# A one-core hybrid decoder step: the pairs' weight halves divided between GpSimd and VectorE, half of the convolutions moved to the down stage, and another border in front of the pairs

## The chip, the core and the metric

The kernel runs on one core of a Trainium2 chip. The core has a TensorE (PE, with its weight load shown as PEld), a VectorE (DVE), a ScalarE (ACT), a GpSimd (POOL) and a SyncE (SP), which issues nearly all transfers. Each engine takes its instructions in program order and waits on semaphores for the others. The metric is the device time of one execution in microseconds (us); lower is better.

## The reference, cut to what matters

One layer of a decoder over 1056 tokens: 1024 of a prompt and 8 sequences of 4. All data is float32. The part that the change touches is the last third, the feed-forward block with its causal depthwise convolution of width 3:

```python
def _conv_ffn(h, cbuf, w_up, b_up, conv_w, conv_b, w_down, b_down):
    L = h.shape[1]
    u = h @ w_up + b_up                                  # 1024 -> 5632
    ux = jnp.concatenate([cbuf.astype(u.dtype), u], axis=1)
    y = conv_b + ux[:, 0:L] * conv_w[0]
    for j in range(1, CONV_W):
        y = y + ux[:, j:j + L] * conv_w[j]
    a, g = y[..., :D_FF], y[..., D_FF:]                  # D_FF = 2816
    out = (jax.nn.gelu(a) * g) @ w_down + b_down         # 2816 -> 1024
    return out, ux[:, L:]
...
    h2 = _ln(x) * (1.0 + sc2) + sh2
    f, cbuf_new = _conv_ffn(h2, cbuf, w_up, b_up, conv_w, conv_b, w_down, b_down)
    x = _ln(ALPHA * x + g2 * f, ln2_g, ln2_b)
```

Ahead of it stand the input projection, the mLSTM, the windowed attention, the gated merge and the output projection, which the change leaves alone.

## The kernel before

**Number format.** A float32 operand is split into a rounded high part and a low part, and each product is three matmuls: high by high, high by low, low by high. The high part is a cast on ScalarE, the low part a subtraction on VectorE or GpSimd. So each block of weights costs a cast and a subtraction before TensorE can use it.

**Layout.** Activations lie as tiles of 128 features by 1056 tokens. There are 43 such tiles ("slots") on the chip, handed out and given back in order of age. A product over 1056 tokens is made in three pieces of 384, 384 and 288 tokens, each in one of three accumulation banks (L), which ScalarE or VectorE empties.

**The up stage.** The 44 column blocks of `w_up` (128 columns each) belong in twos: block j (it goes through gelu) and block 22 + j (it multiplies). Some are made directly (`up_direct`, 24 matmuls for each piece of tokens). The others go through `fast`: for a pair of blocks, a Strassen-like scheme with seven half-size products (numbered 1 to 7) in place of eight. Each product is 12 matmuls of 264 tokens for each of two halves of the tokens, so a pair is 168 matmuls. Products go to a ring of eight accumulation banks; VectorE adds them into the two output tiles (`fdst`), and ScalarE copies out product 1. The operands of the scheme, sums and differences of the activation's quarters, are made once ahead of the first pair (`tprep`, `t1_split`). The sums and differences of the weights are made for each pair: four sums of 128x512 (`sum`, L1447), seven casts (`high`, L1464), seven low parts (`low`, L1468). In this kernel the sums and all seven low parts are GpSimd's.

**Before and after the pairs.** Three pairs of blocks (j = 0, 1, 2) are made directly in front of the pairs, two (j = 20, 21) behind them, and 17 pairs go through the scheme. `history` loads the convolution's old inputs and transposes them; it runs between the direct blocks and the pairs.

**Convolutions.** `conv` takes one tile: a ScalarE pass (L1746), two VectorE passes over the prompt's tokens (L1750, L1752), and small operations for the sequences on VectorE (L1755 to L1757), ScalarE and GpSimd (L1748, L1758, L1759). In the pairs' stage `post` does both convolutions of each pair, gelu (L1773), the product (L1776), and stores one finished tile. For the five direct j, the raw tiles are stored, and the convolutions are made later.

**The down stage.** Chunks (one j, 128 rows of `w_down`) are taken in five groups (`KG`). `feed` loads a chunk, makes what is not yet made of it, and splits it into high (L1842) and low (L1844). `down_group` multiplies a group with its weights and adds into eight accumulators (`facc`, L1959; in the first group ScalarE writes them, L1957). The weights' low parts are GpSimd's here. The fourth group goes by pieces of tokens (`down_by_tokens`), so that finished rows are transposed and added to the residual (`pre`, L1898); the last group is multiplied row by row with the final norm (L2124 on).

**What sets the order.** The order is written by a planner at build time. Each three matmuls call `pulse(us)`, which moves a planner's clock forward. Side work (`tprep`, `post`, `feed`, ...) is written as generators in one queue (`sides`); `rate` says how many steps of the generator in front are taken for each planner's microsecond. `later(us, f)` issues f that much later. `operands(gi)` stands in front of each group: if the group's chunks are not yet made, it takes the steps of the queue at once, with no matmul between them.

Of the kernel before, what the change touches and what calls it, by code (L numbers as in the profile page):

```python
# [19 lines left out]
SEQ = 1024  # L20
# [13 lines left out]
RATE_T, RATE_U, RATE_V, RATE_D, RATE_P = 0.85, 0.75, 0.8, 0.8, 0.9  # L34
# [70 lines left out]
def hybrid_step(ctx: ExitStack, tc: tile.TileContext, I, O):  # L105
# [1265 lines left out]
    def tprep():  # L1371

        for kp in range(4):
# [4 lines left out]
            yield  # L1378
            e, o = quarters(hf[2 * kp]), quarters(hf[2 * kp + 1])
            S.dma_start(b12D[kp], e[:, :, 1, :])  # L1380
            V.tensor_tensor(e[:, :, 0, :], e[:, :, 1, :], e[:, :, 0, :], op=OP.subtract)
            yield
            V.tensor_tensor(e[:, :, 1, :], o[:, :, 1, :], e[:, :, 1, :], op=OP.subtract)
            V.tensor_tensor(o[:, :, 1, :], o[:, :, 1, :], e[:, :, 0, :], op=OP.subtract)
            yield
            V.tensor_tensor(o[:, :, 0, :], o[:, :, 0, :], o[:, :, 1, :], op=OP.subtract)
            t_ops[kp] = slot(F32R, name="thi"), slot(F32R, name="tlo")
            A.copy(t_ops[kp][0], hf[2 * kp + 1])
# [8 lines left out]
            V.tensor_tensor(t3_ops[kp][1], e[:, :, 1, :], t3_ops[kp][0].bitcast(F32), op=OP.subtract)
# [23 lines left out]
    class Pair:  # L1421
# [44 lines left out]
        def low(self, p):  # L1466
            hi, lo = self.halves(p)
            G.tensor_tensor(lo, self.src[p], hi.bitcast(F32), op=OP.subtract)  # L1468
# [272 lines left out]
    def conv(c, u, y):  # L1741
# [3 lines left out]
        us = tiny([128, 8, 6], "us", 6)  # L1745
        A.activation(y[:, :SEQ], u[:, :SEQ], AF.Identity, bias=b, scale=w[2])  # L1746
        A.copy(us[:, :, 2:6], to3(u[:, SEQ:]))
        G.tensor_copy(us[:, :, 0:2], aux["hist"][:, :, :, c])  # L1748
# [5 lines left out]
        ys = to3(y[:, SEQ:])  # L1754
        V.tensor_scalar(ys, us[:, :, 2:6], w[2], b, op0=OP.mult, op1=OP.add)  # L1755
        V.scalar_tensor_tensor(ys, us[:, :, 1:5], w[1], ys, op0=OP.mult, op1=OP.add)
        V.scalar_tensor_tensor(ys, us[:, :, 0:4], w[0], ys, op0=OP.mult, op1=OP.add)  # L1757
# [448 lines left out]
```

## Time and profile before

| | |
|---|---|
| time, median of 3 runs | 2018.43 us (2017.61 to 2020.57) |
| the profiled execution's own time | 2016.51 us |
| its span | 2014.8 us |
| busy: PE, DVE, ACT, POOL | 1914.2, 1085.8, 775.3, 670.7 us |
| mean granted clock of TensorE | 0.988 |
| data read, written | 165.74 MB, 53.49 MB |

The page splits the span in 40 slices of some 50 us. The up stage begins near 1150 us; the pairs run from about 1259 to 1666 us, the down stage from about 1720 us to the end. TensorE is busy nearly throughout, so the places to look at are the ones where it isn't: these have a row with an idle time in brackets in the timeline of TensorE, or less than the stretch's length in the table of windows.

### The profile page before, as it was taken

The numbers are of one execution on the slowest core, as the hardware profiler recorded it, in microseconds if no ns is written. First come the engines' busy times: TensorE is split into PE (matmuls) and PEld (weight loads), VectorE is DVE, ScalarE is ACT, GpSimd is POOL, SyncE is SP. The second block draws the span as 40 slices with busy tenths as digits, with TensorE's granted clock in tenths as the row PEclk, the third lists the DMA queues.
The fourth block names the chain that finished last, engine by engine and source line by source line (L and its number), as shares of the span: only waits on it lengthen the run. The fifth ranks groups of instructions, "written<-read, shape, count | busy, mean of one in ns | idle before, by whom it ended". The sixth has DMA issues, their size and how long they took to land. (4 is left out here: it accounts for less than half of the span.)

```text
span 2014.8 us, 33111 instructions
## 1 busy us (share of the span) xinstructions
PE 1914.2 (95%) x13005; PEld 1818.0 (90%) x13005; DVE 1085.8 (54%) x2281; ACT 775.3 (38%) x1613; POOL 670.7 (33%) x806
## 2 busy tenths in 40 slices
PE   6999999999999999999999999798988999999987
PEld 4899999999998999988999988788888889999975
DVE  5454444354643635312553566677777775315778
ACT  5444334343655555410322454233333334431331
POOL 2013324140213122000000442578887870222327
PEclk9999999999999999999999999899999999999999
DMA  9152423515121322695424142212222125323373
GB/s 285 46 148 24 128 69 83 121 31 133 33 86 43 100 65 65 219 346 175 131 64 115 74 128 95 66 64 75 74 65 75 64 75 180 119 95 114 108 246 131
DMA packets 230981, 219.35 MB, mean 109 GB/s; under 512 B 11377, under 2 KB 207137, under 8 KB 230793
## 3 DMA queue, kind: packets, MB, share of 16 engines
q1 hardware_dynamic: 230045, 216.63, 35.3%
q8 instruction: 102, 1.67, 0.4%
q10 hardware_dynamic: 780, 0.61, 0.1%
q14 instruction: 54, 0.44, 0.1%
HBM read 165.74 MB, written 53.49 MB: 109 GB/s over the span
## 5 line engine op out<-in xcount | busy, mean ns | idle before, releaser
L454 PE MATMUL L<-hhi,whi 128*128 128x384 f32 (+1 forms) x1600 | 525.7, 329 | 0.1
L454 PE MATMUL L<-hlo,whi 128*128 128x384 f32 (+1 forms) x1600 | 516.4, 323 | 0.0
L454 PE MATMUL L<-hhi,wlo 128*128 128x384 f32 (+1 forms) x1600 | 516.0, 322 | 0.0
L454 PEld LDWEIGHTS L<-hhi,whi 128*128 128x128 f32 x1600 | 301.0, 188 | 6.6 <-issue 4.8
L454 PEld LDWEIGHTS L<-hlo,whi 128*128 128x128 f32 x1600 | 301.4, 188 | 0.3
L454 PEld LDWEIGHTS L<-hhi,wlo 128*128 128x128 f32 x1600 | 300.9, 188 | 0.0
L432 DVE TENSOR_TENSOR wlo<-wraw,whi 128x1024 fp32r<-128x1024 f32 (+1 forms) x87 | 107.0, 1230 | 111.0 <-ACT whi L428 110.0
L454 PE MATMUL L<-mhi,whi 128*128 128x384 f32 (+1 forms) x432 | 144.2, 334 | 11.8 <-ACT u L1737 5.5
L299 POOL TENSOR_SCALAR rstd<-mv 128x1 f32<-128x1 f32 (+1 forms) x36 | 22.0, 610 | 398.3 <-DVE mv L308 374.9
L454 PE MATMUL L<-mhi,wlo 128*128 128x384 f32 (+1 forms) x432 | 141.8, 328 | 0.4 <-DVE wlo L432 0.4
L454 PE MATMUL L<-ahi,whi 128*128 128x384 f32 (+1 forms) x432 | 140.9, 326 | 1.0 <-DVE facc L1959 0.9
L454 PE MATMUL L<-mlo,whi 128*128 128x384 f32 (+1 forms) x432 | 141.8, 328 | 0.1
L454 PE MATMUL L<-ahi,wlo 128*128 128x384 f32 (+1 forms) x432 | 139.7, 323 | 1.8 <-POOL wlo L432 1.8
L454 PE MATMUL L<-alo,whi 128*128 128x384 f32 (+1 forms) x432 | 139.4, 323 | 0.0
L1468 POOL TENSOR_TENSOR fw<-fsum,fw 128x512 fp32r<-128x512 f32 x68 | 105.2, 1548 | 76.5 <-ACT fw L1464 76.5
L432 POOL TENSOR_TENSOR wlo<-wraw,whi 128x768 fp32r<-128x768 f32 (+2 forms) x27 | 53.7, 1995 | 193.4 <-ACT whi L428 167.7
L428 ACT CAST whi<-wraw 128x1024 fp32r<-128x1024 f32 (+2 forms) x114 | 113.4, 996 | 3.6 <-DMA wraw<-in_w_in 2.2
L454 PEld LDWEIGHTS L<-mhi,whi 128*128 128x128 f32 x432 | 83.1, 192 | 14.5 <-ACT u L1737 6.8
L1750 DVE SCALAR_TENSOR_TENSOR y<-fdst,vT,y 128x1023 f32<-128x1023 f32 x34 | 43.7, 1284 | 82.3 <-ACT y L1746 80.9
L1494 PE MATMUL L<-mhi,fw 128*128 128x264 f32 x400 | 79.1, 286 | 9.1 <-POOL fw L1468 9.1
L1464 ACT CAST fw<-fsum 128x512 fp32r<-128x512 f32 x68 | 41.9, 616 | 112.0 <-POOL fsum L1447 110.9
L454 PEld LDWEIGHTS L<-mhi,wlo 128*128 128x128 f32 x432 | 83.0, 192 | 0.9 <-DVE wlo L432 0.9
(538 smaller groups left out, 4446.4 us busy)
## 6 DMA issues: line engine op xcount, KB each, us to landing
wraw<-in_w_in SPq DMA_DIRECT2D x52, 512.0 KB
wada<-in_w_ada SPq DMA_DIRECT2D x44, 512.0 KB
fraw<-in_w_up SPq DMA_DIRECT2D x34, 512.0 KB
ld<-ff SPq DMA_DIRECT2D x27, 528.0 KB
ff<-y SPq DMA_DIRECT2D x17, 528.0 KB
wraw<-in_w_down SPq DMA_DIRECT2D x88, 64.0 KB
ff<-u SPq DMA_DIRECT2D x10, 528.0 KB
wraw<-in_w_up SPq DMA_DIRECT2D x10, 512.0 KB
```

Source lines behind the costliest of these rows:

```text
L299: G.tensor_scalar(r[:n], var, eps, None, op0=OP.add)
L428: A.copy(hi[:, :n], t[:, :n])
L432: self.low_by.tensor_tensor(lo[:, :n], t[:, :n], hi[:, :n].bitcast(F32), op=OP.subtract)
L454: T.matmul(ps[:, :nt], x[:, c], y[:, t0:t0 + nt], start=i == 0, stop=i == last)
L1464: A.copy(hi, self.src[p])
L1468: G.tensor_tensor(lo, self.src[p], hi.bitcast(F32), op=OP.subtract)
L1494: T.matmul(ps, x, y, start=kp == 0 and i == 0, stop=kp == 3 and i == 2)
L1750: V.scalar_tensor_tensor(y[:, 1:SEQ], u[:, :SEQ - 1], w[1], y[:, 1:SEQ], op0=OP.mult, op1=OP.add)
```

## The change

- **Weights of the pairs.** GpSimd keeps the four sums and the low parts of products 1 and 4; VectorE takes the low parts of products 2, 3, 5, 6 and 7.
- **Convolutions.** In the pairs' stage only block 22 + j is convolved and stored (`yD`). Block j is stored raw (`uD`) and is convolved in the down stage, where `feed` now loads two tiles for every chunk and does gelu and the product for all 22. In `conv`, the four small operations of GpSimd and one of VectorE become ScalarE's.
- **Border in front of the pairs.** Four pairs of blocks are direct ahead of the scheme instead of three, and 16 pairs go through it. `tprep` is written so that the cast and the low parts of one step stand behind the next step's sums; `history` is run inside it.
- **Groups.** The down stage's groups have 5, 5, 5, 3 and 4 chunks instead of 6, 5, 4, 3 and 4. `feed` is one generator over all of them; it starts a chunk only if at least `ROOM` = 9 slots are free, and the rates of the planner are others.

```diff
-RATE_T, RATE_U, RATE_V, RATE_D, RATE_P = 0.85, 0.75, 0.8, 0.8, 0.9
+RATE_T, RATE_U, RATE_V, RATE_D, RATE_P = 0.5, 0.5, 1.1, 1.1, 1.1
+ROOM = 9
...
-    ND, NE = 3, 2
+    ND, NE = 4, 2
...
-    KG = [6, 5, 4, 3, 4]
-    chunks_of = [[3, 4, 5, 6, 7, 8], [9, 10, 11, 12, 0], [13, 14, 15, 1], [16, 2, 20], [17, 18, 19, 21]]
+    KG = [5, 5, 5, 3, 4]
+    chunks_of = [[4, 5, 6, 7, 8], [9, 10, 11, 0, 20], [12, 13, 14, 1, 21], [2, 15, 16], [3, 17, 18, 19]]
...
+        for kp in range(5):
+            if kp < 4:
+                join(kp)
+            yield
+            if kp:
+                high(kp - 1)
+            if kp < 4:
+                e, o = quarters(hf[2 * kp]), quarters(hf[2 * kp + 1])
+                S.dma_start(b12D[kp], e[:, :, 1, :])
+                V.tensor_tensor(e[:, :, 0, :], e[:, :, 1, :], e[:, :, 0, :], op=OP.subtract)
+                V.tensor_tensor(e[:, :, 1, :], o[:, :, 1, :], e[:, :, 1, :], op=OP.subtract)
+            yield
+            if kp < 4:
+                V.tensor_tensor(o[:, :, 1, :], o[:, :, 1, :], e[:, :, 0, :], op=OP.subtract)
+                V.tensor_tensor(o[:, :, 0, :], o[:, :, 0, :], o[:, :, 1, :], op=OP.subtract)
+            yield
+            if kp:
+                low(kp - 1)
             yield
...
         def low(self, p):
             hi, lo = self.halves(p)
-            G.tensor_tensor(lo, self.src[p], hi.bitcast(F32), op=OP.subtract)
+            (G if p in (1, 4) else V).tensor_tensor(lo, self.src[p], hi.bitcast(F32), op=OP.subtract)
...
+        ys = to3(y[:, SEQ:])
         A.activation(y[:, :SEQ], u[:, :SEQ], AF.Identity, bias=b, scale=w[2])
         A.copy(us[:, :, 2:6], to3(u[:, SEQ:]))
-        G.tensor_copy(us[:, :, 0:2], aux["hist"][:, :, :, c])
+        A.activation(ys, to3(u[:, SEQ:]), AF.Identity, bias=b, scale=w[2])
+        A.copy(us[:, :, 0:2], aux["hist"][:, :, :, c])
+        A.copy(aux["ucol"][:, c, 0:2], u[:, SEQ - 2:SEQ])
+        A.copy(aux["ucol"][:, c, 2:18].rearrange("p (b j) -> p b j", b=8), to3(u[:, SEQ:])[:, :, 2:4])
...
-        V.tensor_scalar(ys, us[:, :, 2:6], w[2], b, op0=OP.mult, op1=OP.add)
...
-        G.tensor_copy(aux["ucol"][:, c, 0:2], u[:, SEQ - 2:SEQ])
-        G.tensor_copy(aux["ucol"][:, c, 2:18].rearrange("p (b j) -> p b j", b=8), us[:, :, 4:6])
...
     def post(c, u):
         y = slot(name="y")
         yield from conv(c, u, y)
         drop(u)
...
+        to_dram(yD, c, y)
...
+    def feed():
+        js, got = [j for c in chunks_of for j in c], {}
+        def load(n):
+            if n < len(js) and n not in got:
+                ds = [uD[js[n]], yD[22 + js[n]] if 22 + js[n] in yD else uD[22 + js[n]]]
+                got[n] = [slot(name="ld") for _ in ds]
+                for t, d in zip(got[n], ds):
+                    S.dma_start(t, d)
+        load(0)
+        yield
+        for n, j in enumerate(js):
+            while len(free_slots) < ROOM:
+                yield
+            load(n + 1)
+            yield
+            u, y2 = got.pop(n)
+            if 22 + j not in yD:
+                u2, y2 = y2, slot(name="y")
+                yield from conv(22 + j, u2, y2)
+                drop(u2)
+                yield
+            y = slot(name="y")
+            yield from conv(j, u, y)
...
+            A.activation(y, y, AF.Gelu_apprx_tanh)
+            yield
+            yield
+            V.tensor_tensor(y, y, y2, op=OP.mult)
...
+            A.copy(hi, y)
+            yield
+            V.tensor_tensor(lo, y, hi.bitcast(F32), op=OP.subtract)
...
+            if n == 9:
+                yield from gate_rows2()
+        yield from kept_rows()
...
     def ff_finisher(j):
-        return lambda blk_, z: sides.append(post(22 * blk_ + j, z))
+        return lambda blk_, z: sides.append(post(22 + j, z)) if blk_ else to_dram(uD, j, z)
...
-        sums = tprep()
-        for i in range(23):
-            if i == 5:
+        sums, past = tprep(), history()
+        for i in range(22):
+            if i in (0, 5, 10):
+                next(past)
+            if i == 6:
                 upairs[0].load()
-            if i in (10, 11, 22):
-                upairs[0].step((10, 11, 22).index(i) - 3)
+            if i in (15, 20):
+                upairs[0].step((15, 20).index(i) - 3)
             else:
-                next(sums)
-            yield
-        next(sums, None)
+                next(sums, None)
+            yield
+        upairs[0].step(-1)
```

Three places show what the change does to the order. First GpSimd, over one pair in the middle of the pairs' stage; `fsum` are sums of weights, `fw` the weights in two parts, `fraw` the weights as loaded. Before:

```order
L1447 TENSOR_TENSOR fsum_12968<-fraw_12799,fraw_12800 128x512
L1447 TENSOR_TENSOR fsum_12968<-fraw_12799,fsum_12931 128x512
L1758 COPY ucol_12337<-fdst_12815 128x2
L1759 COPY ucol_12337<-us 128x16
L1468 TENSOR_TENSOR fw_12971<-fraw_12799,fw_12971 128x512
L1748 COPY us<-cst 128x8x2
L1468 TENSOR_TENSOR fw_13008<-fsum_12968,fw_13008 128x512
L1468 TENSOR_TENSOR fw_13042<-fsum_12931,fw_13042 128x512
L1758 COPY ucol_12337<-fdst_12740 128x2
L1759 COPY ucol_12337<-us 128x16
L1468 TENSOR_TENSOR fw_13078<-fraw_12800,fw_13078 128x512
L1468 TENSOR_TENSOR fw_13113<-fsum_12968,fw_13113 128x512
```

and with the change, a whole pair (the line numbers are the changed kernel's):

```order
L1460 TENSOR_TENSOR fsum_14007<-fraw_13885 128x512
L1460 TENSOR_TENSOR fsum_14007<-fsum_14007,fraw_13884 128x512
L1460 TENSOR_TENSOR fsum_14047<-fraw_13884,fraw_13885 128x512
L1460 TENSOR_TENSOR fsum_14047<-fraw_13884,fsum_14007 128x512
L1481 TENSOR_TENSOR fw_14151<-fraw_13885,fw_14151 128x512
L1481 TENSOR_TENSOR fw_14209<-fraw_14117,fw_14209 128x512
```

A pair has gone from eleven large operations and six small ones on GpSimd to six large ones.

Second, VectorE of the changed kernel at the border between the second and the third group of the down stage. L1963 is the addition into the accumulators (each waits for a block of matmuls), L1767 to L1772 the convolution, L1864 the product behind gelu, L1870 the chunk's low part:

```order
L1963 TENSOR_TENSOR facc_17192<-L_72,facc_17192 128x288
L1767 SCALAR_TENSOR_TENSOR y_17843<-ld_17628,vT,y_17843 128x1023
L1769 SCALAR_TENSOR_TENSOR y_17843<-ld_17628,vT,y_17843 128x1022
L1771 SCALAR_TENSOR_TENSOR y_17843<-us,vT,y_17843 128x32
L1772 SCALAR_TENSOR_TENSOR y_17843<-us,vT,y_17843 128x32
L1767 SCALAR_TENSOR_TENSOR y_17855<-ld_17627,vT,y_17855 128x1023
L1769 SCALAR_TENSOR_TENSOR y_17855<-ld_17627,vT,y_17855 128x1022
L1771 SCALAR_TENSOR_TENSOR y_17855<-us,vT,y_17855 128x32
L1772 SCALAR_TENSOR_TENSOR y_17855<-us,vT,y_17855 128x32
L1864 TENSOR_TENSOR y_17855<-y_17855,y_17843 128x1056
L1870 TENSOR_TENSOR alo_17870<-y_17855,ahi_17869 128x1056
L1963 TENSOR_TENSOR facc_16654<-L_73,facc_16654 128x384
```

The whole last chunk of the third group, with both its convolutions, now stands between the last addition of one group and the first of the next. Before, additions of both groups follow each other there:

```order
L1959 TENSOR_TENSOR facc_17388<-L_71,facc_17388 128x384
L1959 TENSOR_TENSOR facc_17388<-L_72,facc_17388 128x288
L1959 TENSOR_TENSOR facc_16848<-L_73,facc_16848 128x384
```

Third, VectorE at the border between the fourth and the last group; `PG` is the first bank of the final products, L2133 the first operation that reads one:

```order
L1963 TENSOR_TENSOR facc_17192<-L_72,facc_17192 128x288
L1998 TENSOR_TENSOR facc_17192<-facc_17192,modT 128x32
L1767 SCALAR_TENSOR_TENSOR y_18886<-ld_18565,vT,y_18886 128x1023
L1769 SCALAR_TENSOR_TENSOR y_18886<-ld_18565,vT,y_18886 128x1022
L1771 SCALAR_TENSOR_TENSOR y_18886<-us,vT,y_18886 128x32
L1772 SCALAR_TENSOR_TENSOR y_18886<-us,vT,y_18886 128x32
L1864 TENSOR_TENSOR y_18886<-y_18886,ld_18566 128x1056
L1870 TENSOR_TENSOR alo_18901<-y_18886,ahi_18900 128x1056
L2133 TENSOR_TENSOR PG<-PG,gp_17267 128x512
```

Before, the first final product's rows follow the last addition directly. With the change, the last chunk's work stands in between.

More of the change, by code (lines that the diff above doesn't have):

```diff
@@ L1371, in tprep, with join @@
     def tprep():
-        for kp in range(4):
+        def join(kp):
             for k in (2 * kp, 2 * kp + 1):
@@ L1806, in hybrid_step, with kept_rows @@
     acts2 = []
-    def feed(gi):
-        js, got = chunks_of[gi], {}
+    def kept_rows():
+        ucol = aux["tile"]
+        uo = slot(name="uo")
+        for _ in range(4):
+            yield
+        for i in range(7):
+            n = 128 if i < 6 else 24
+            transpose(pd(i)[:n], ucol[:, i * 128:i * 128 + n])
+        A.copy(uo[:, :512], PD[0])
+        A.copy(uo[:, 512:768], PD[1][:, :256])
+        A.copy(uo[:24, 768:896], PD[1][:24, 256:384])
+        drop(ucol)
+        yield
+        for i in range(7):
+            n = 128 if i < 6 else 24
+            r0 = i * 128
+            for dst, a, b in (("p_conv", 0, 88), ("s_conv", 88, 792)):
+                p, q = max(r0, a), min(r0 + n, b)
+                if p < q:
+                    S.dma_start(dap(O[dst], (p - a) * 128, [[128, q - p], [1, 128]]),
+                                uo[p - r0:q - r0, i * 128:(i + 1) * 128])
+        drop(uo)
+        yield
+    def feed():
+        js, got = [j for c in chunks_of for j in c], {}
         def load(n):
             if n < len(js) and n not in got:
-                ds = [aD3[js[n]]] if js[n] in aD3 else [uD[js[n]], uD[22 + js[n]]]
+                ds = [uD[js[n]], yD[22 + js[n]] if 22 + js[n] in yD else uD[22 + js[n]]]
                 got[n] = [slot(name="ld") for _ in ds]
@@ L1831, in feed @@
                 yield
-                yield from conv(j, u, y)
-                drop(u)
-                yield
-                A.activation(y, y, AF.Gelu_apprx_tanh)
-                yield
-                yield
-                V.tensor_tensor(y, y, y2, op=OP.mult)
-                drop(y2)
-                yield
+            y = slot(name="y")
+            yield from conv(j, u, y)
+            drop(u)
+            yield
[3 more added lines that the diff above has]
+            V.tensor_tensor(y, y, y2, op=OP.mult)
+            drop(y2)
+            yield
             hi, lo = slot(F32R, "ahi"), slot(F32R, "alo")
@@ L1904, in pre @@
             drop(*facc)
-            sides.append(kept_rows())
     summed = []
@@ L1962, in down_group @@
         a = operands(gi)
-        sides.append(feed(gi + 1))
         for j in range(8):
@@ L1977, in down_by_tokens @@
         a = operands(gi)
-        sides.append(feed(gi + 1))
         for ti in range(3):
@@ L2060, in hybrid_step @@
     finish_sides()
-    sides.append(history())
     rate[0] = RATE_U
@@ L2079, in hybrid_step @@
     fast(upairs, up_end)
-    sides.append(feed(0))
+    sides.append(feed())
     rate[0] = RATE_V
```

63 lines of the change are left out of this document (6 added, 57 removed).

## The prediction

> **What bounds the kernel now.** I read the page first, then a table of windows cut at the stages' borders, then the chain of waits within the slow stages.
>
> ```profile
> span 2014.8 us, 33111 instructions
> ...
> 1210.00:1258.80 48.80, 44.43 (x275) 41.54 (x274) 32.67 (x50) 21.93 (x39) 10.54 (x10) 0.97 0.28 96
> 1258.80:1282.30 23.50, 10.19 (x58) 8.86 (x57) 15.83 (x17) 8.42 (x16) 9.99 (x7) 0.64 0.30 94
> ...
> 1300.00:1650.00 350.00, 317.58 (x2545) 311.23 (x2543) 262.08 (x375) 122.46 (x211) 278.82 (x252) 1.00 0.21 69
> ...
> 1673.40:1890.00 216.60, 216.60 (x1340) 216.45 (x1341) 89.92 (x121) 73.75 (x104) 47.54 (x46) 0.99 0.36 117
> 1890.00:1960.00 70.00, 58.54 (x342) 53.14 (x341) 47.22 (x72) 26.60 (x41) 19.27 (x13) 0.95 0.64 220
> ```
>
> The columns are the stretch, its length, the busy time of PE, PEld, DVE, ACT, POOL, the granted clock, the DMA share and GB/s. From 1673 to 1890 us, TensorE has no gap: it bounds the down stage, and VectorE has 127 us to spare. In the pairs (1300 to 1650) it lacks 32 us while GpSimd is busy for 279 of 350. In front of the pairs (1259 to 1282) it works 10 of 23.5 us, at 0.64 of its clock.
>
> What sets the pace of a pair is in the chain of waits and in the groups of that stretch:
>
> ```profile
> 1279.29 3.01 PE PD L1494 x12
> ...
> 1291.03 2.90 PE PD L1494 x24
> 1293.93 1.46 PE PE L1494 x12
> 1295.39 4.39 PE L L1494 x36
> 1299.78 1.50 PE PF L1494 x12
> ...
> 1341.71 1.30 POOL fw L1468
> ...
> 1364.96 1.29 POOL fw L1468
> ...
> 1673.39 116.82 PE L L454 x714
> ```
>
> ```profile
> L1468 POOL TENSOR_TENSOR fw<-fsum,fw 128x512 fp32r<-128x512 f32 x60 | 93.1, 1551 | 70.0 <-ACT fw L1464 70.0
> L1447 POOL TENSOR_TENSOR fsum<-fraw,fraw 128x512 f32<-128x512 f32 x15 | 34.3, 2286 | 0.0
> L1447 POOL TENSOR_TENSOR fsum<-fraw 128x512 f32<-128x512 f32 x15 | 19.2, 1279 | 0.0
> ...
> L1752 DVE SCALAR_TENSOR_TENSOR y<-fdst,vT,y 128x1022 f32<-128x1022 f32 x30 | 62.5, 2083 | 0.5
> L1750 DVE SCALAR_TENSOR_TENSOR y<-fdst,vT,y 128x1023 f32<-128x1023 f32 x30 | 38.5, 1284 | 78.9 <-ACT y L1746 78.9
> L1517 DVE SCALAR_TENSOR_TENSOR fdst<-L,vT,fdst 128x264 f32<-128x264 f32 x47 | 21.8, 485 | 0.4
> ```
>
> The same low part comes back every 23.25 us (1341.71 to 1364.96), which is the period of a pair. Where nothing holds it up, TensorE does 72 matmuls between 1291.03 and 1299.78, 0.1215 us each, so a pair's 168 need 20.4 us. GpSimd, which casts on ScalarE wait for and which waits for casts, costs 2.85 us in each pair. VectorE and GpSimd also slow each other: the two equal passes L1750 and L1752 take 1.28 and 2.08 us, the equal sums 1.28 and 2.29.
>
> **The pairs and the border in front.** First and last matmuls of this stage, and TensorE's waits around its start:
>
> ```profile
> L1494 PE MATMUL L<-mhi,fw x400: 278/284/391, 1283.6 to 1665.8; 128*128 128x264 f32 x134
> ...
> L1494 PE MATMUL PF<-mhi,fw x144: 278/285/393, 1258.8 to 1658.6; 128*128 128x264 f32 x144
> ```
>
> ```profile
> 1246.28 0.44 PE L454 MATMUL L<-mhi,whi 128*128 128x384 f32 x1 [0.95 <-ACT u L1737]
> ...
> 1253.98 0.40 PE L454 MATMUL L<-mhi,whi 128*128 128x288 f32 x1 [3.22 <-ACT u L1737]
> 1268.26 0.59 PE L1494 MATMUL PD<-thi,fw 128*128 128x264 f32 x1 [5.29 <-ACT thi L1388]
> ...
> 1277.13 1.62 PE L197 MATMUL PD<-cst,hraw 128*128 128x128 f32 x6 [6.77 <-DVE fdst L1504]
> ```
>
> The stage takes 1665.8 - 1258.8 = 407.0 us for 17 pairs, stalls at its start included. With the change GpSimd has six large operations a pair, at most 6 x 2.29 = 13.7 us, against a period of 20.4. VectorE loses one convolution, gelu's product and a small operation and gains five low parts. None of 512 columns stands on it yet; one of 528 does:
>
> ```profile
> 1236.25 0.70 DVE L1397 TENSOR_TENSOR tl<-hf,th 128x528 fp32r<-128x528 f32 x1
> ...
> 1859.29 0.25 DVE L1756 SCALAR_TENSOR_TENSOR y<-us,vT,y 128x32 f32<-128x32 f32 x1
> ```
>
> So 14 additions of 0.485 (6.8), five low parts of 0.70 (3.5), two passes of 1.28 (2.6), two small ones (0.5): 13.4 us. If each of the seven longer ones were slowed by 0.8 like L1752, it is 19. Both are under 20.4, so TensorE sets the pace. Of the waits this adds, the tightest is product 6's low part: it stands behind product 4's addition, with that pair's convolution behind it, and is wanted two products of 2.9 us later. In the 16 pairs, 16 x 20.4 = 326.4 us. The pair that becomes direct is 144 matmuls at 116.82/714 = 0.1636: 23.6. Together 350.0, a gain of **57.0**. For filling the first pair I take back **2**; the bounds are 0 and today's 13.6 us (5.29, 6.77, and the 1.55 by which twelve matmuls took 3.01 instead of 1.46 behind them). I stay near 0, since `tprep` and `history` now stand under three direct blocks. ScalarE's waits on `tprep` (0.95 and 3.22) go with the new spacing: **4.2**, at worst 0, if its casts of `fw` block the evacuations as today.
>
> **The down stage.** It makes 28 convolutions in place of 10, and 22 gelus and products in place of 5. Durations of each there, from the timelines of ScalarE and VectorE:
>
> ```profile
> 1822.20 1.09 ACT L1835 ACTIVATE y<-y 128x1056 f32<-128x1056 f32 x1 [17.03 <-DVE y L1757]
> ...
> 1825.44 1.25 DVE L1838 TENSOR_TENSOR y<-y,y 128x1056 f32<-128x1056 f32 x1
> 1826.77 1.08 ACT L1842 CAST ahi<-y 128x1056 fp32r<-128x1056 f32 x1 [2.86 <-DVE y L1838]
> 1827.70 0.56 DVE L1959 TENSOR_TENSOR facc<-L,facc 128x384 f32<-128x384 f32 x1 [1.02 <-PE L L454]
> 1828.17 1.25 DVE L1844 TENSOR_TENSOR alo<-y,ahi 128x1056 fp32r<-128x1056 f32 x1
> ...
> 1846.88 1.24 ACT L1746 ACTIVATE y<-ld,vT 128x1024 f32<-128x1024 f32 x1 [6.36 <-PE L L454]
> ...
> 1855.23 1.27 DVE L1750 SCALAR_TENSOR_TENSOR y<-ld,vT,y 128x1023 f32<-128x1023 f32 x1
> ```
>
> A convolution is 2 x 1.27 + 2 x 0.25 = 3.0 us on VectorE. Eighteen more and 17 more products of 1.25 are 76 us; with the 89.9 there it stays far under the stage, so in the mean it hides behind the matmuls. A chunk's own chain is 1.24 + 3.0 + 1.09 + 1.25 + 1.08 = 7.7, with hand-overs some 8.3 us. The planner gives it ten steps at 1.1, 9.1 of its microseconds. Its clock counts 1.32 for nine matmuls, which take 9 x 0.1636 = 1.47, so that is 10.1 us: enough. The loads double to two tiles a chunk, 1.08 MB in 10 us, 107 GB/s beside today's 117; 220 is reached a stage later.
>
> What doesn't hide are the group borders where the order has chunk work with no matmul between (the places shown with the change). The wait for nine free tiles puts them there: the feed idles until a group's tiles come back.
>
> - Up to first group: gelu, product, cast and low part of the fifth chunk stand behind the last evacuation: 1.09 + 1.25 + 1.08 + 1.25 = 4.7 us. The four ready chunks cover 12 matmuls, 2.0; with the evacuation and hand-overs **+4** (0 to 5).
> - First to second group: the last part is issued just in time. **+2** (0 to 6).
> - Second to third: an addition of 0.56, two convolutions 6.0, then the 4.7. That is 11.3 less 2.0, so 9.3, and behind such a gap the slow start costs 1.55 as above: **+11** (4, if VectorE is ahead, to 14).
>
> ```profile
> 1943.40 10.29 DMA x1r<-x1D
> ...
> 1954.46 1.97 PE L197 MATMUL PD<-cst,facc 128*128 128x128 f32 x8 [6.08 <-DVE x1r L1898]
> ...
> 1972.01 2.77 PE PE L2124 x12
> ```
>
> - Fourth to last (rows of the chain and of TensorE's timeline above): here ScalarE is tied to TensorE too: 0.56 + 1.24 + 3.0 + 4.7 = 9.5, less nine matmuls of 2.77/12 (2.1): 7.4. But TensorE already waits 6.08 a little later for a transfer of 10.29 us issued at this border, which the new wait covers. **+3** (0 to 8).
> - Fourth group and the gate rows' transposes: **+1** (0 to 4).
>
> The Trainium skill ("TensorE: Matmul & The Clock Gate", What's actually happening) has the clock at half after an idle window of about 3.4 us, until a busy one of that length. By it all three gaps named here would cost about 1.7 us each, an estimate, and the sum would be some 3 us higher. The trace agrees for one gap, with its 1.55 and the clock of 0.64 in that stretch; for gaps of 4 us it shows nothing.
>
> Sum: -57.0 + 2 - 4.2 + 4 + 2 + 11 + 3 + 1 = **-38.2**. From the profiled execution's 2016.5 (1.7 of it around the span) that is 1978.3. The median of the runs shown stands 1.9 above that execution, so I forecast **1980 us**, with its own range from 1964 to 1996.
>
> **Rivals.**
>
> - *The feed becomes the bound of the down stage: 2000.* A group of five chunks has eight of GpSimd's low parts beside it, 1.6 a chunk, and each chunk four additions in VectorE's queue. The passes show what meeting GpSimd costs, 0.8 us, and an addition costs 0.56: the chain would go from 8.3 to 8.3 + 1.3 + 2.2 = 11.8, over 10.1. Part of the additions falls into VectorE's waits for ScalarE; I price 1.2 us on each of 17 chunks, 20 us. Against it: ten convolutions went under the matmuls before without any gap. The Trainium skill ("SBUF — State Buffer", Who interferes with whom) says that a VectorE operation with two inputs on chip and a reading GpSimd operation exclude each other for a whole instruction. By that a meeting could cost a whole 1.28, 0.5 more, and the rival would stand some 13 us higher, an estimate. The trace agrees that they collide, with 0.8 on average.
> - *The pairs don't reach TensorE's pace: 2004.* Low parts on VectorE stand in line behind additions that wait for TensorE; if a chain over both holds the period near 22, that is 1.5 us on 16 pairs, 24 us. For: today's period is such a ring. Against: of the 5.8 us at the tightest place, the convolution's pass and the low part take 2.
> - *No stops at the borders: 1962.* VectorE and ScalarE work ahead of the matmuls and most of the 18 us falls away. The order speaks against: the operations stand behind the last additions.
> - *Slower, 2038.* Additions queue behind convolutions, the three banks fill, and none of the 76 us more on VectorE is hidden; with it today's gain is eaten (1980 + 76 - 18). It decides once more than two blocks' time, 2 x 15 x 0.1636 = 4.9 us, of other work stands between two additions all along. Away from the borders the order has at most one convolution there, 3.0.
>
> **How the numbers follow.** Forecast 0.61, feed-bound 0.20, pairs short 0.08, no stops 0.08, slower 0.03. About 0.2% (4 us) is what a measurement of this kernel tells from no change. All but the last lie far below 2014, and the last above 2022: faster 0.96, same 0.01, slower 0.03. The range of 1960 to 2003 takes in the rival without stops, the unknown prices, and the greater part of the two rivals at 2000 and 2004.
>
> **What would show it.** Right: pairs 20.4 to 20.8 us apart and TensorE without gaps in them, the granted clock near 1.00 in front of them; GpSimd busy less than half there; in the down stage gaps of TensorE at the borders only, the longest, 8 to 11 us, in front of the third group, ended by VectorE or ScalarE making `alo` or `ahi`. Wrong: many short gaps on L454 ended by additions to `facc` (feed-bound), waits of the pairs for `fw` made on VectorE, or a stall left where `thi` is made.

## The result and the profile after

| | before | after |
|---|---|---|
| time, median of 4 runs each | 2019.5 us | **1970.82 us** (1968.38 to 1972.52) |
| ratio, 95% interval | | 0.9758 (0.9741 to 0.9775) |
| the profiled execution: time, span | 2016.51, 2014.8 us | 1968.38, 1966.7 us |
| busy DVE, ACT, POOL | 1085.8, 775.3, 670.7 us | 1074.7, 805.7, 473.5 us |

The change takes 2.4% off. Between the two profiled executions it is 48.1 us, where the sum had 38.2. Line numbers below are those of the changed kernel, unless a row is of another one.

First the table of windows of the changed kernel (stretch, its length, busy time of PE, PEld, DVE, ACT, POOL, granted clock, DMA share, GB/s): in front of the pairs, in the pairs, in the down stage, around its third group, and at the end.

```profile
1260.00:1283.00 23.00, 23.00 (x156) 23.00 (x155) 12.97 (x12) 8.34 (x16) 7.14 (x5) 1.00 0.19 75
1302.00:1562.00 260.00, 260.00 (x2140) 260.00 (x2139) 165.27 (x295) 80.30 (x185) 104.13 (x78) 1.00 0.32 106
1675.00:1785.00 110.00, 104.71 (x654) 104.18 (x652) 76.52 (x89) 60.11 (x125) 25.51 (x14) 0.99 0.37 117
1785.00:1800.00 15.00, 11.67 (x56) 11.27 (x57) 11.69 (x15) 7.37 (x17) 3.80 (x2) 0.73 0.40 125
1895.00:1960.00 65.00, 53.01 (x230) 40.48 (x230) 54.16 (x81) 13.12 (x13) 37.91 (x36) 0.92 0.47 174
```

In front of the pairs TensorE worked 10 of 23.5 us at 0.64 of its clock; now it is busy throughout at 1.00. In the pairs it has no gap, and GpSimd is busy 40% of the time.

The matmuls of this stage by tile, first and last start, and the groups of GpSimd and VectorE in it:

```profile
L1507 PE MATMUL PF<-mhi,fw x128: 278/284/293, 1278.6 to 1583.4; 128*128 128x264 f32 x128
...
L1507 PE MATMUL L<-mhi,fw x384: 278/284/293, 1285.9 to 1605.3; 128*128 128x264 f32 x192
```

```profile
L1481 POOL TENSOR_TENSOR fw<-fraw,fw 128x512 fp32r<-128x512 f32 x26 | 33.7, 1312 | 162.0 <-ACT fw L1477 162.0
...
L1481 DVE TENSOR_TENSOR fw<-fsum,fw 128x512 fp32r<-128x512 f32 x51 | 40.5, 794 | 0.0
...
L1769 DVE SCALAR_TENSOR_TENSOR y<-fdst,vT,y 128x1022 f32<-128x1022 f32 x13 | 16.6, 1275 | 0.0
L1767 DVE SCALAR_TENSOR_TENSOR y<-fdst,vT,y 128x1023 f32<-128x1023 f32 x12 | 15.4, 1285 | 15.9 <-ACT y L1760 15.9
```

From 1278.6 to 1605.3 us the 16 pairs take 326.7 us, 20.4 each. GpSimd now waits 162 us of 260 for ScalarE's casts: that wait is slack. The two passes of the convolution take the same 1.28 us; the second was 2.08 before.

Then TensorE's waits from 1600 us on (what waited, for whom, us in total, times, the longest), and its timeline at the border between second and third group:

```profile
PE L L455 <- ACT ahi L1868: 12.0, 2, 8.0
PE PG L2125 <- ACT ahi L1868: 7.1, 1, 7.1
...
PE L L455 <- DVE alo L1870: 1.5, 2, 0.9
```

```profile
1787.72 0.69 PE L455 MATMUL L<-ahi,whi 128*128 128x384 f32 x1 [8.01 <-ACT ahi L1868]
1789.02 0.69 PE L455 MATMUL L<-alo,whi 128*128 128x384 f32 x1 [0.60 <-DVE alo L1870]
1789.50 0.52 PE L455 MATMUL L<-ahi,wlo 128*128 128x384 f32 x1
1789.82 0.52 PE L455 MATMUL L<-ahi,whi 128*128 128x384 f32 x1
...
1793.30 0.33 PE L455 MATMUL L<-ahi,wlo 128*128 128x384 f32 x1
1793.47 0.34 PE L455 MATMUL L<-ahi,whi 128*128 128x384 f32 x1
```

The long gaps lie at the borders: 3.96 and 0.86 in front of the first group (the rest of the 12.0 and 1.5), 8.01 and 0.60 in front of the third, 7.07 in front of the last. Behind the longest, twelve matmuls come every 0.32 us instead of 0.175, 1.7 us more.

### The profile page after: what moved, and what is told of

Read it like the earlier page. It is cut to its first block, busy times and chain, and to the rows that moved or that the text cites. A ratio compares the mean times of both kernels' runs of the same rounds, so it can differ in the third digit from the quotient of the medians.

```text
span 1966.7 us, 33071 instructions
## 1 busy us (share of the span) xinstructions
PE 1907.2 (97%) x12981; PEld 1818.7 (92%) x12981; DVE 1074.7 (55%) x2305; ACT 805.7 (41%) x1792; POOL 473.5 (24%) x587
## 5 line engine op out<-in xcount | busy, mean ns | idle before, releaser
L455 PE MATMUL L<-mhi,whi 128*128 128x384 f32 (+1 forms) x480 | 158.4, 330 | 5.6 <-DVE r L1697 3.0
L455 PE MATMUL L<-mhi,wlo 128*128 128x384 f32 (+1 forms) x480 | 155.9, 325 | 0.5 <-DVE wlo L433 0.5
L455 PE MATMUL L<-mlo,whi 128*128 128x384 f32 (+1 forms) x480 | 155.7, 324 | 0.0
L433 POOL TENSOR_TENSOR wlo<-wraw,whi 128x640 fp32r<-128x640 f32 (+2 forms) x31 | 60.0, 1938 | 240.7 <-ACT whi L429 209.3
L1481 POOL TENSOR_TENSOR fw<-fraw,fw 128x512 fp32r<-128x512 f32 x32 | 42.9, 1353 | 239.0 <-ACT fw L1477 239.0
L455 PEld LDWEIGHTS L<-mhi,whi 128*128 128x128 f32 x480 | 90.9, 189 | 7.5 <-DVE r L1697 3.3
L455 PEld LDWEIGHTS L<-ahi,whi 128*128 128x128 f32 x432 | 82.3, 190 | 13.8 <-ACT ahi L1868 12.6
L455 PEld LDWEIGHTS L<-mhi,wlo 128*128 128x128 f32 x480 | 90.7, 189 | 1.0 <-DVE wlo L433 1.0
L455 PEld LDWEIGHTS L<-mlo,whi 128*128 128x128 f32 x480 | 91.0, 189 | 0.1
L455 PEld LDWEIGHTS L<-alo,whi 128*128 128x128 f32 x432 | 82.4, 191 | 2.1 <-DVE alo L1870 2.1
```

The lines of the kernel that those rows point to most:

```text
L433: self.low_by.tensor_tensor(lo[:, :n], t[:, :n], hi[:, :n].bitcast(F32), op=OP.subtract)
L455: T.matmul(ps[:, :nt], x[:, c], y[:, t0:t0 + nt], start=i == 0, stop=i == last)
L1481: (G if p in (1, 4) else V).tensor_tensor(lo, self.src[p], hi.bitcast(F32), op=OP.subtract)
```

## The experiments

Twelve kernels ran. A kernel's own time is given (the kernel before took 2019.5 to 2022.0 us beside them), and its ratio to the kernel before on the same chip with the 95% interval; "period" is the distance of the same GpSimd sum from one pair to the next between 1310 and 1560 us.

| kernel | us | ratio (interval) | period |
|---|---|---|---|
| before | 2019.5 | 1 | 23.27 |
| the change | 1970.8 | 0.9758 (0.9741 to 0.9775) | 20.42 |
| low parts back on GpSimd | 1970.3 | 0.9754 (0.9740 to 0.9769) | 20.45 |
| before + low parts on VectorE | 1987.3 | 0.9841 (0.9826 to 0.9856) | 21.30 |
| both convolutions in the pairs | 1969.9 | 0.9752 (0.9736 to 0.9768) | 20.59 |
| of the change in the pairs, only half the convolutions | 1975.5 | 0.9773 (0.9755 to 0.9790) | 20.43 |
| before + small operations on ScalarE | 2008.0 | 0.9938 (0.9923 to 0.9952) | 22.53 |
| low parts on GpSimd, two VectorE passes more | 1973.3 | 0.9760 (0.9741 to 0.9779) | 20.45 |
| low parts on GpSimd, one ScalarE pass more | 1973.1 | 0.9762 (0.9746 to 0.9778) | 20.40 |
| old order in front of the pairs | 1977.0 | 0.9789 (0.9772 to 0.9806) | |
| ROOM 7 and other rates | 1960.2 | 0.9709 (0.9694 to 0.9723) | |
| ... and `x1r` fetched ahead | **1950.6** | 0.9653 (0.9638 to 0.9667) | |
| ... and one VectorE pass more per chunk | 1976.6 | 0.9782 (0.9766 to 0.9797) | |
| ... and three direct pairs | 1961.0 | 0.9703 (0.9686 to 0.9720) | |

### Which part sets the pairs free

The change does three things to a pair: low parts to VectorE, one convolution (with the gelu and the product behind it) out of the stage, small operations to ScalarE. I first undid the part that names the change.

```diff
-            (G if p in (1, 4) else V).tensor_tensor(lo, self.src[p], hi.bitcast(F32), op=OP.subtract)
+            G.tensor_tensor(lo, self.src[p], hi.bitcast(F32), op=OP.subtract)
```

> The changed kernel with all seven low parts of a pair on GpSimd again, all else as changed (one convolution a pair, small copies on ScalarE). Theory (the low parts on VectorE set the pace free): GpSimd has eleven large operations again, 14 to 18 us, and the 2.85 us for which casts and low parts wait for each other; a pair takes 21.5 to 23 us, 16 x 1.1 to 2.6 = 18 to 42 us more: 1988 to 2012. Rival (the convolution that left and the small copies did it): pairs stay below 20.7 us apart, 1970 to 1976.

Measured: no difference; the rival held. The window of the pairs and two groups of this kernel:

```profile
1310.00:1560.00 250.00, 250.00 (x2058) 250.00 (x2057) 132.54 (x222) 78.62 (x182) 182.14 (x136) 1.00 0.31 103
```

```profile
L1481 POOL TENSOR_TENSOR fw<-fsum,fw 128x512 fp32r<-128x512 f32 x49 | 73.3, 1506 | 29.9 <-ACT fw L1477 27.4 <-DMA ff<-y 2.5
...
L1460 POOL TENSOR_TENSOR fsum<-fraw,fraw 128x512 f32<-128x512 f32 x13 | 16.8, 1291 | 0.0
```

GpSimd has eleven large operations again, but none of its sums takes 2.29 us any more. It is busy 182 of 250 us (14.9 a pair) and still has some of its waits to spare. So the low parts on VectorE are not needed once the other two parts are in. Are they enough alone? The same line, put into the kernel before:

```diff
-            G.tensor_tensor(lo, self.src[p], hi.bitcast(F32), op=OP.subtract)
+            (G if p in (1, 4) else V).tensor_tensor(lo, self.src[p], hi.bitcast(F32), op=OP.subtract)
```

> The kernel before with one line changed: low parts of products 2, 3, 5, 6 and 7 on VectorE. Both convolutions, gelu and its product stay in the pairs. Theory (the low parts alone set the pace free): VectorE has 13.4 + 4.3 = 17.7 us a pair, pairs come 20.4 to 20.9 us apart instead of 23.25, 17 x 2.35 to 2.85 = 40 to 48 less than before: 1971 to 1980. Rival (VectorE needs the room that half the convolutions leave): additions and low parts queue behind the convolutions' passes, pairs 21.8 to 23.5 apart: 1995 to 2022.

Measured: 33 us less, 21.30 a pair, between the two expectations. This window tells why it stops there:

```profile
1310.00:1560.00 250.00, 246.80 (x1983) 242.37 (x1982) 230.59 (x351) 94.59 (x165) 152.23 (x141) 1.00 0.23 75
```

VectorE is busy 92%, 19.6 us a pair where I had 17.7: the low parts of sums took 1.11 us and both passes of the convolution 1.69 to 1.82. That is still less than TensorE's 20.4, and the next kernel holds TensorE's pace with VectorE just as busy, so its busy time alone is not the bound. The chain of waits from 1334 to 1357 us goes round, from one pair to the next, over GpSimd's low part and sums, ScalarE's cast, a low part on VectorE and the passes of both convolutions; a quarter of it is time that the profile puts down to no operation. So the ring now runs over three engines, and what closes it at 21.30 is not shown. Then both convolutions, gelu and the product back into the changed kernel's pairs:

```diff
+        if c >= 22:
+            ya[c - 22] = y
+            yield
+            return
+        yield
+        A.activation(y, y, AF.Gelu_apprx_tanh)
...
+        V.tensor_tensor(y, y, ya[c], op=OP.mult)
+        drop(ya.pop(c))
+        to_dram(aD3, c, y)
...
-        return lambda blk_, z: sides.append(post(22 + j, z)) if blk_ else to_dram(uD, j, z)
+        return lambda blk_, z: sides.append(post(22 * blk_ + j, z))
```

In this kernel the feed ends earlier, so that the transposes of the convolution's kept inputs (`kept_rows`) fall between the transposes of one tile of rows in `pre` and the addition that reads the same banks; that tile gets other values, and the work is the same.

> The changed kernel with both convolutions, gelu and the product of each pair made in the pairs' stage again (rate of the planner there 0.75 for 0.5); the down stage convolves only the six direct pairs. Low parts and border stay as changed. Theory (with the low parts shared VectorE has room for it): 17.7 us a pair on VectorE, pairs stay 20.4 to 20.8 apart; of the stops in the down stage the one in front of the first group goes (4.8), the one in front of the third, which is forced in the order again, stays: 1963 to 1968. Rival (the moved convolution is what lets VectorE keep up): pairs 21.5 to 22.5 apart, 18 to 34 more: 1984 to 2000.

```profile
1310.00:1560.00 250.00, 250.00 (x2051) 249.40 (x2050) 232.12 (x342) 113.01 (x266) 113.18 (x72) 1.00 0.25 78
```

Measured: VectorE is busy 93%, 19.1 us a pair, and TensorE has no gap; a pair takes 20.59. So the convolution need not leave either. In the down stage the 4.8 us in front of the first group went, as expected, but 4.3 us on `fdst` came at the border behind the pairs: the total is that of the change, 2 us above the range expected. Next, of the three parts only the convolution that left, with gelu and product (low parts on GpSimd, small operations where they were):

```diff
-            (G if p in (1, 4) else V).tensor_tensor(lo, self.src[p], hi.bitcast(F32), op=OP.subtract)
+            G.tensor_tensor(lo, self.src[p], hi.bitcast(F32), op=OP.subtract)
...
-        A.copy(us[:, :, 0:2], aux["hist"][:, :, :, c])
+        G.tensor_copy(us[:, :, 0:2], aux["hist"][:, :, :, c])
...
+        G.tensor_copy(aux["ucol"][:, c, 0:2], u[:, SEQ - 2:SEQ])
+        G.tensor_copy(aux["ucol"][:, c, 2:18].rearrange("p (b j) -> p b j", b=8), us[:, :, 4:6])
```

> The changed kernel with all low parts on GpSimd and the convolution's small operations as before (three on GpSimd, one more on VectorE): of the change in the pairs only the convolution that left remains. Theory (one convolution less is enough: GpSimd's sums no longer meet VectorE's passes): GpSimd 14.65 us a pair as in the run with the low parts on it, plus 0.73 for three small operations, 15.4; with 4.7 of waits for casts, the amount of the kernel before, 20.1, just under TensorE's 20.4: no change, 1967 to 1974. Rival (small operations wait for ScalarE or VectorE and hold up the sums behind them): 21 to 22 a pair, 1980 to 1996.

Measured: the pairs keep 20.43 without a gap, as the theory has it. The 5 us that the kernel is longer, 1.5 us over the range expected, don't lie there; its waits for `ahi` are 2.2 and 0.8 us longer in the down stage and at the last border. Last, the small operations alone, in the kernel before, by the same edit to `conv` as in the change:

> The kernel before with only the convolution's small operations moved to ScalarE. Low parts on GpSimd, both convolutions in the pairs. Theory (busy time and waits of GpSimd's ring add up): 18.5 busy less 1.46 for six small operations, plus 4.7 of waits, 21.8 us a pair for 23.25: 17 x 1.45 = 25 less, 1990 to 2000. Rival 1 (the small operations are in GpSimd's slack): no change, 2016 to 2023. Rival 2 (they are what closes the ring): full pace, 1971 to 1980.

Windows and one group of GpSimd in this kernel:

```profile
1310.00:1560.00 250.00, 233.48 (x1872) 229.04 (x1872) 187.36 (x256) 103.89 (x243) 192.30 (x122) 1.00 0.22 71
```

```profile
L1468 POOL TENSOR_TENSOR fw<-fsum,fw 128x512 fp32r<-128x512 f32 x44 | 63.0, 1433 | 56.8 <-ACT fw L1464 56.8
...
L1447 POOL TENSOR_TENSOR fsum<-fraw,fraw 128x512 f32<-128x512 f32 x11 | 25.2, 2287 | 0.0
```

Measured: 2008.0 us, between two of the expectations, and 22.53 a pair, half of the gain expected. GpSimd's busy time fell by the 1.4 us that it should (192.30/250 x 22.53 = 17.3), but its waits for casts rose from 4.6 to 5.1. The ring of sum, cast and low part was still closed, and part of what one member gave, another took.

What of the second convolution closes it? Two kernels add one half of it to the base with the low parts on GpSimd.

```diff
         yield from conv(c, u, y)
+        for _ in range(2):
+            yield
+            V.scalar_tensor_tensor(y[:, 2:SEQ], u[:, :SEQ - 2], 0.0, y[:, 2:SEQ], op0=OP.mult, op1=OP.add)
         drop(u)
```

> The changed kernel with the low parts on GpSimd (1970.3 us, pairs 20.45 apart), and in each pair two more VectorE passes over 1022 columns behind the convolution, which add zero times the tile. VectorE has again about what the second convolution had, but ScalarE has nothing of it. Theory (GpSimd's sums take 2.28 instead of 1.29 us where they meet VectorE's passes, and that closes the ring): two sums a pair at 2.28 again, GpSimd 14.65 + 2.0, with 4.7 of waits 21.4 us a pair, 16 x 0.95 = 15 more: 1980 to 1996. Rival (the second convolution's place in ScalarE's queue, ahead of the casts, closed the ring): pairs stay at 20.5, 1968 to 1975.

```diff
+    def pass_on(c, u):
+        A.activation(u[:, :SEQ], u[:, :SEQ], AF.Identity)
+        yield
+        to_dram(uD, c, u)
+        yield
...
-        return lambda blk_, z: sides.append(post(22 + j, z)) if blk_ else to_dram(uD, j, z)
+        return lambda blk_, z: sides.append(post(22 + j, z) if blk_ else pass_on(j, z))
```

> The same base (low parts on GpSimd, 1970.3 us), and in each pair one more ScalarE pass of 1.24 us over block j's finished tile, in place, where the second convolution's ScalarE pass stood; no VectorE work. Theory (collisions of VectorE and GpSimd close the ring): pairs stay at 20.5, 1968 to 1975. Rival (ScalarE's pass waits for VectorE's last addition and holds the casts behind it): GpSimd's waits for casts rise above the 5.6 us a pair that are slack now, pairs 21.3 to 22.5 apart, 14 to 33 more: 1984 to 2003.

Measured: both keep the period (20.45 and 20.40), and neither is told apart from its base. ScalarE's pass alone is thus excluded in this base, where GpSimd's waits for casts stay as they were (64.3 and 65.4 of 250 us). The other run misses its mark: in it the sums stay at 1.29 us, as this row of GpSimd's groups shows, so the collision that it was to bring back didn't take place, and it says nothing on what one would cost.

```profile
L1460 POOL TENSOR_TENSOR fsum<-fraw,fraw 128x512 f32<-128x512 f32 x12 | 15.5, 1292 | 0.0
```

What in the second convolution closed the ring (its passes where they meet the sums, gelu behind them in ScalarE's queue, or both) stays open. The kernel before points to gelu for the longest of GpSimd's three waits in a pair. Rows of ScalarE and of GpSimd there, one wait after the other:

```profile
1403.38 1.09 ACT L1773 ACTIVATE y<-y 128x1056 f32<-128x1056 f32 x1 [4.60 <-DVE y L1757]
1404.38 0.60 ACT L1464 CAST fw<-fsum 128x512 fp32r<-128x512 f32 x1
1405.06 1.86 POOL L1468 TENSOR_TENSOR fw<-fsum,fw 128x512 fp32r<-128x512 f32 x1 [2.45 <-ACT fw L1464]
...
1419.65 1.24 ACT L1746 ACTIVATE y<-fdst,vT 128x1024 f32<-128x1024 f32 x1 [3.98 <-DVE fdst L1517]
1420.91 0.62 ACT L1464 CAST fw<-fsum 128x512 fp32r<-128x512 f32 x1
1421.61 1.76 POOL L1468 TENSOR_TENSOR fw<-fsum,fw 128x512 fp32r<-128x512 f32 x1 [1.44 <-ACT fw L1464]
```

The casts for which GpSimd waits 2.45 and 1.44 us stand behind gelu and behind a convolution's pass, which themselves wait for VectorE; the third wait is 0.58. No run took gelu alone out of the pairs, so this is a pointer and not a proof.

### The border in front of the pairs

```diff
-        sums, past = tprep(), history()
-        for i in range(22):
-            if i in (0, 5, 10):
-                next(past)
...
+        sums = tprep()
+        for i in range(23):
...
     finish_sides()
+    sides.append(history())
```

with `tprep` as it was before, and four direct pairs as in the change:

> The changed kernel with the border in front of the pairs written as before (operands of the scheme and the first pair's weights in the old order, the old inputs' transposes behind the direct blocks), but still four direct pairs. Theory (the order there made the stalls): 5.3 on `thi`, 6.8 in front of the transposes, 1.55 of slow start and up to 4.2 of ScalarE's waits come back: 13 to 18 more, 1983 to 1990. Rival (two more direct blocks give cover enough, whatever the order): below 4 more, 1969 to 1975.

TensorE's waits from 1200 to 1300 us in this kernel:

```profile
PE PD L198 <- DVE fdst L1505: 3.0, 1, 3.0
...
PE PD L1495 <- DVE cst L1785: 0.5, 1, 0.5
```

Measured: 1977.0 us, 6 more than the change, between the two expectations; the intervals of the two ratios overlap by a hair. Nothing waits for `thi` any more, though the order is the old one; the stall in front of the transposes is back, 3.0 and 0.5, with the 1.6 us of transposes behind it. The other half, the new order with three direct pairs, on the best kernel below:

```diff
-RATE_T, RATE_U, RATE_V, RATE_D, RATE_P = 0.5, 0.5, 1.25, 1.2, 1.1
+RATE_T, RATE_U, RATE_V, RATE_D, RATE_P = 0.9, 0.5, 1.25, 1.2, 1.1
-    ND, NE = 4, 2
+    ND, NE = 3, 2
```

> The same kernel (1950.6 us) with three direct pairs in front of the scheme in place of four, 17 pairs in the scheme, and the planner's rate there 0.9 for 0.5, so that the scheme's operands are still made under the direct blocks, in the new order. A pair in the scheme takes 20.4 and a direct one 23.6. Theory (the new order alone is enough): 3.2 less, 1945 to 1949. Rival (the fourth pair is the cover that `tprep` needs): `thi`, `tlo` or the weights of the first pair are late and TensorE waits 5 to 12 us in front of the pairs: 1952 to 1960.

```profile
PE PD L1507 <- ACT fw L1477: 5.7, 1, 5.7
PE PD L1507 <- DVE fw L1481: 2.8, 1, 2.8
```

Measured: 10.4 us more. The first pair's weights are late by 5.7 and 2.8 us: squeezed under two direct blocks less, the operands and the weights of the first pair don't get done. So the fourth direct pair is worth more than the 3.2 us that it costs, at the one rate tried, and the new order is worth the 3.5 us of stall that came back, and likely the 6 us measured.

### The stops in the down stage

```diff
-RATE_T, RATE_U, RATE_V, RATE_D, RATE_P = 0.5, 0.5, 1.1, 1.1, 1.1
-ROOM = 9
+RATE_T, RATE_U, RATE_V, RATE_D, RATE_P = 0.5, 0.5, 1.25, 1.2, 1.1
+ROOM = 7
```

> The changed kernel with ROOM 7 for 9 and the planner's rates 1.25, 1.2, 1.1 for 1.1, 1.1, 1.1: in the order, no step of the feed stands in front of a group without matmuls between. Theory (the stops at the borders come from chunk work that is forced there): TensorE's waits in front of the first group (4.8 us) and of the third (8.6 us, and some 1.5 of slow start behind it) go; in front of the last group the 7.1 us on `ahi` go, and the wait of about 6 us on `x1r` that it covered comes back. That is 4.8 + 10.1 + 1.1 = 16 less: 1955 us, 1951 to 1960. Rival (the chunk chain is short of time, and the stops only gather it): short gaps ended by `ahi`, `alo` or additions to `facc` appear inside the groups and add up to as much: 1966 to 1973.

```profile
PE PD L198 <- DVE x1r L1927: 10.3, 3, 6.2
PE L L455 <- ACT ahi L1868: 3.1, 1, 3.1
```

Measured: 10.7 us less. The gaps in front of the third and the last group are gone, the one in front of the first shrank to 3.1 and 0.7, and inside the groups no addition came later than 0.5 us. But the wait for the residual rows, which the stop at the last border had covered, came back larger than the 6 that I gave it: 10.3 in three places. It is a load that is issued too late. With one dictionary over all three pieces of tokens, the fetch ahead crosses their borders:

```diff
+    x1s, got1 = {}, set()
...
         for i in ids:
-            n, x = rows_of(i), xs_[i]
+            n, x = rows_of(i), x1s[i]
             fetch(i + 1)
...
-            if i in ids:
-                xs_[i] = slot(name="x1r")
+            if i < 9 and i not in got1:
+                got1.add(i)
+                x1s[i] = slot(name="x1r")
```

> The kernel with ROOM 7 and the other rates (1960.2 us), and in it the residual rows `x1r` of a token piece's first tile are fetched while the last tile of the piece ahead is added. Theory (TensorE's 10.3 us on `x1r` come from loads that are issued too late): 6 to 10 less, 1950 to 1955. Rival (the transfers at this place fill the queues at 300 to 420 GB/s, an earlier request only displaces another): 1957 to 1962.

```profile
PE L L455 <- ACT ahi L1868: 2.6, 1, 2.6
PE PD L198 <- DVE x1r L1929: 1.9, 2, 1.6
PE PD L198 <- ACT facc L1997: 1.2, 2, 0.9
```

Measured: 1950.6 us, 9.6 less; of the 10.3 us on `x1r` 1.9 are left. This version beats both kernels, by 3.5% and 1.0%.

Is the feed near its bound there? Its chain got one VectorE pass more for each chunk:

```diff
+            V.scalar_tensor_tensor(y[:, 2:SEQ], y2[:, :SEQ - 2], 0.0, y[:, 2:SEQ], op0=OP.mult, op1=OP.add)
             A.activation(y, y, AF.Gelu_apprx_tanh)
```

> The kernel with ROOM 7, the other rates and `x1r` fetched ahead (1950.6 us), and in each of the 22 chunks one more VectorE pass of 1.3 us between the convolution and gelu (it adds zero times the other tile). Theory (a chunk's chain has room under the matmuls, but for the five chunks of the first group, which are made one behind the other from the end of the pairs on): 5 x 1.3 = 6.5 more in front of the first group and up to 1.5 elsewhere, 1954 to 1960. Rival (the feed is near the bound everywhere): 1.3 on each of the 17 chunks behind these too, 1974 to 1982.

```profile
PE L L455 <- DVE facc L1966: 7.4, 8, 2.1
PE L L455 <- ACT ahi L1869: 6.6, 1, 6.6
PE PD L198 <- DVE gt L1883: 3.0, 1, 3.0
```

Measured: 26 us more for 22 x 1.3 = 28.6 us of work. Hardly any of it is hidden; my theory fell. The wait in front of the first group grew by 4.0 of the expected 6.5, and inside the groups additions to `facc` now come late in eight places. In front of the three longest (2.06, 1.81 and 1.63 us), VectorE's order has the chunk's product and its low part, which wait for gelu and for the cast on ScalarE; from one addition to the next that is 4.4 to 4.9 us (timeline of VectorE). Without the added pass three such places have 4.1 to 4.4 us, and TensorE waits only 0.5 us for `facc`. The listed waits grew by about 16 us. Of the rest, one part lies in the clock, which is 0.95 to 0.99 in stretches where it was 1.00; the remainder I can't place.

## Why the prediction was right, and where it was off

The time (1970.8) lay in the forecast's own range. By its steps, between the two profiled executions:

- **Pairs, -57.0, +2 and -4.2.** Right. The stage took 326.7 us for 16 pairs (326.4 in the sum). It starts 1278.6 - 1258.8 = 19.8 us later than before, 1.9 of which come from far ahead, so that 17.9 + 326.7 stands against 407.0: -62.4, where the three terms make -59.2. The first pair filled without any wait, so the +2 was too careful, and ScalarE's two waits went. With them went 1.4 us that the sum left out: behind the wait of 3.22 us the matmuls of the kernel before came at half pace (rows in the last section). VectorE is busy 165.27/260 x 20.42 = 13.0 us a pair; I had 13.4.
- **But not for the reason given.** The working relieved GpSimd by moving its low parts. Taking them back costs nothing, and the convolution that left, with its gelu, frees the pairs alone. The mechanism (a ring over GpSimd and casts that closes above TensorE's pace) fits all of this: every relief lowered the period, the convolution alone to 20.43, the low parts alone to 21.30, the small operations alone to 22.53. It is argued from the waits, though: 42% of the chain of waits over a pair of the kernel before (1336 to 1361 us) is put down to no operation. That one part suffices and another brings two thirds, the prediction didn't see; its step put the whole gain on GpSimd's six large operations. The size came out all the same because TensorE's 20.4 caps what any of them can bring.
- **Border up-direct to group 1, +4.** 4.8 us and about 1.3 of slow start. What the sum left out is the border one step ahead: TensorE's wait behind the last pair fell from 2.7 to 0.7.
- **Group 1 to 2, +2.** No gap at all.
- **Group 2 to 3, +11.** 8.01 + 0.60 + 1.7 = 10.3, at the place named and ended by the operations named.
- **Fourth group to last, +3.** A wait of 7.07 took the place of the 6.08: +1. That it covers the wait for `x1r` was shown when it was taken away and that one came back.
- **Fourth group, +1.** Its small waits fell from 5.2 to 2.8, -2.4: 1.5 of them on `x1r` are 0.5 now, and 1.9 on `facc` are gone.

Sum of what was measured: 1.9 - 62.4 - 2.0 + 6.1 + 10.3 + 1 - 2.4 = -47.5, against 48.1 in the profiled executions. The 9 us between the two sums are thus four terms too careful by 2 to 3.4 us (pairs, group 1 to 2, last border, fourth group) and a border that wasn't counted; the first group's term, 2.1 short, and the 1.9 from far ahead go the other way.

Of the rivals: the pairs that don't reach TensorE's pace didn't happen in the change, but in the kernel before with the same low parts on VectorE they did, at 21.3. The rival in which the feed becomes the bound was nearer than its 0.20: the prediction gave a chunk's chain 8.3 us of 10.1, and an added 1.3 us, which should have fitted, cost 26 us, 1.2 a chunk in the mean. This was in the faster kernel with ROOM 7; the change itself has no such gaps inside its groups. That step of the working was wrong. The chain of waits of the changed kernel shows it: from the end of the pairs to the first group it runs through the feed, some 10 us for each chunk (here the first VectorE pass of every second one).

```profile
1612.45 1.30 DVE y L1767
...
1633.19 1.29 DVE y L1767
...
1652.24 1.30 DVE y L1767
```

The slower rival was to decide once 4.9 us of other work stand between two additions all along, and the working counted one convolution there, 3.0. It overlooked the product and the low part, which with their waits for ScalarE stand between two additions for up to 4.1 us in the changed kernel, and for up to 4.9 with the added pass, where additions are late in places.

The Trainium skill ("TensorE: Matmul & The Clock Gate", What's actually happening) had the clock at half behind an idle window of about 3.4 us, and would have had all three border gaps cost slow time. The trace agrees for all three: nine matmuls come every 0.32 us behind the gap of 3.96 us, which the prediction left open, twelve behind the one of 8.01, and behind the 7.07 matmuls of 512 columns come every 0.43 us instead of 0.23 until 1905.8 us. The prediction said that the trace of the kernel before shows nothing for gaps of 4 us, but it shows half pace behind 3.22 and 3.04 us.

## What to carry to other kernels

When an engine's ring sets the pace and a faster bound lies just below, try each relief alone: the smallest that gets under the bound brings all there is, and the others only move work to where it may show. Room in the mean (here 127 us on VectorE) is no room in a chain, so look where moved work lands for steps that the order forces between two stretches of matmuls, and for waits that such a stop covers and that come back when it goes.

## What the runs showed of the hardware

- The half clock follows gaps shorter than 3.4 us, too. In the kernel before, the first matmuls behind a gap of 3.22 us come every 0.13 us, and from 1.1 us after its end on every 0.24, for 3.1 us (first rows; all of the same shape); behind one of 3.04 us at 1162.52 they come every 0.24 at once. In the kernel with one pass more per chunk, behind another gap of 3.04 us, they start at full pace and fall to half 1.4 us later, for some 3.3 us (second rows; 0.30 and 0.45 are the same shape). The Trainium skill's window in the section just named is longer than these gaps; the measurement decides.

```profile
1254.75 0.29 PE L454 MATMUL L<-mhi,wlo 128*128 128x288 f32 x1
...
1255.07 0.44 PE L454 MATMUL L<-mlo,whi 128*128 128x288 f32 x1
```

```profile
1726.38 1.03 PE L198 MATMUL PD<-cst,gt 128*32 128x128 f32 x8 [3.04 <-DVE gt L1883]
...
1727.52 0.30 PE L455 MATMUL L<-ahi,wlo 128*128 128x288 f32 x1
...
1728.02 0.45 PE L455 MATMUL L<-ahi,wlo 128*128 128x288 f32 x1
...
1731.26 0.34 PE L455 MATMUL L<-ahi,wlo 128*128 128x384 f32 x1
```

- The same operation's time depends on what the other engine does at that moment, not on how busy that engine is in the mean. VectorE's low part of 512 columns took 0.79 us in the change, 1.11 with both convolutions and small operations on GpSimd, and 1.34 with both convolutions and these on ScalarE, though GpSimd was busier in the second (152 of 250 us) than in the third (113). In the second, one at 1351.87 us, where GpSimd stands idle, took 0.68, and one at 1334.89, beside a low part of GpSimd's, 1.77.
